# Norm scales spread by a repeated column, and shifted starts for the weight blocks that move

## The chip, the cores and the metric

One core of one Trainium2 chip runs the whole program. The metric is device time in microseconds (us) of one execution. The engines are TensorE (PE; its weight loads stand apart as PEld), VectorE (DVE), ScalarE (ACT), GpSimd (POOL) and the DMA queues, of which SyncE (SP) issues most.

## What is computed

Two transformer-like blocks run one after the other on 1024 tokens of 1024 channels, all in float32. The parts of the reference that the change touches are the root-mean-square norms and some of the projections:

```python
def rms_norm(x, w):
    xf = x.astype(jnp.float32)
    y = xf * lax.rsqrt(jnp.mean(xf * xf, axis=-1, keepdims=True) + EPS)
    return (y * w.astype(jnp.float32)).astype(x.dtype)
...
    proj = u @ w_in[l]              # first block: one slice, ib, is a value projection
...
    return rms_norm(h, final_norm_w)          # end of the first block
...
    h = rms_norm_2(x, pre1_w[l]) * (1.0 + sc1) + sh1   # start of the second
    z = h @ w_in                    # gv and mv are value projections
...
    y = swiglu_ffn(h, ffn_w_in[l], ffn_w_out[l])
    x = x + (1.0 + gt2) * rms_norm_2(y, post2_w[l])
```

The norm that ends the first block and the norm that starts the second follow each other directly, so the second one's scale depends on the first one's.

## The kernel before

Channels lie on the 128 partitions and tokens along the free axis, in two halves of 512 tokens (`H`). Four phases follow each other: A (first block's mixer), C (its output projection, gate and final norm), B (second block's mixer) and F (its feed-forward part). The order on TensorE is the order in which the code is written. The other engines are ordered by a scheduler.

**Products.** A float32 number is split into a high and a low part, `hi` and `lo`, both stored in the one-pass type `F32R`. A product takes three matmuls into the same bank: high by high, high by low, low by high (`mm3`, and by hand in `vgroup` and `vg`). In the profile `mm<-rh,hi` names the moving operand first and the stationary one second. In most products the weights are stationary in blocks of 128x128, and 512 tokens of activations (`rh`, `rl`) move.

**Blocks that move.** Three kinds of projection want their result with tokens on the partitions: the values `v` (phase A, `vgroup`), `gv` and `mv` (phase B, `vg`). There the activations are stationary in blocks of 128 tokens, and the weights move, 256 columns in a matmul (280 for `gv` of the first pair, which carries 24 columns more). One such group has 8 token blocks x 8 channel blocks x 3 matmuls = 192 matmuls. There are six groups, five of 256 and one of 280 columns, 1152 matmuls in all. The rest of the matmuls of 256 columns stand in phase F and move activations (`ah`, `al`).

**The ring.** `load_split` fetches a block of weights by DMA to `raw`, ACT copies it to `hi`, and DVE subtracts to make `lo`. `hi` and `lo` come from a ring of four buffers each, 128x1024. In the built program each buffer starts at a multiple of 64 bytes.

**Norm scales.** `token_sums` turns a tile of squares (128x512) on TensorE and adds up on DVE, which gives a column of four sums per partition. `rsqrt_cols` makes the scale of them: a `TENSOR_SCALAR` on DVE and a power on POOL (`mhalf` holds -0.5). `to_rows` spreads this column along the free axis on all partitions: DVE multiplies the identity by the column to the tile `dg` (in the profile `C<-ident,...` or `B<-ident,...`, L2597), and TensorE multiplies a matrix of ones by it (`sm<-C,ones`). The matmul is of full float32 and shows as two records. `norms` at the end of phase C needs two scales, one after the other: the second sum has to be multiplied by the first scale twice before its own power. The waits that `yield` stands for put other TensorE work between the steps.

**The end.** The last product of phase F (`XV`, entries 6 and 7) runs over two quarters of the first half, 256 tokens each. `finish` makes the norm of each quarter. There the sums of squares come from matmuls of the squares by one column of ones, five for each of two token blocks. The last call (`tail`) has no other work beside it: the squares, the sums, the power, `to_rows`, four steps of multiply and add on DVE and the output DMAs follow each other.

`warm` issues matmuls of ones by ones into a bank that nobody reads.

Of the kernel before, what the change touches and what calls it, by code (L numbers as in the profile page):

```python
# [8 lines left out]
F32 = mybir.dt.float32  # L9
F32R = mybir.dt.float32r  # L10
U32 = mybir.dt.uint32
AF = mybir.ActivationFunctionType
ALU = mybir.AluOpType
# [3 lines left out]
P = 128  # L17
# [1515 lines left out]
class PhaseC:  # L1533
# [56 lines left out]
    def phase_c(self, yh, yl):  # L1590
# [104 lines left out]
            accum(acc2[half], m, hh, scale=self.col("final_norm_w", m))  # L1695


        wfa = br.tile([P, 8], F32, name="wfa")
        r1 = br.tile([P, NCH], F32, name="r1")
        r2 = br.tile([P, NCH], F32, name="r2")  # L1700
        rb12 = pair(br, "rb12")
        self.x2d = [tc.dram_tile([P, T], F32, name=f"x2d{k}") for k in range(8)]
        x1 = self.x1 = []
# [1 line left out]
        def norms(half):  # L1705
            if not x1:

                self.stt(wfa, self.mods[:, 8:16], 1.0, self.col("pre1_w_2", 0, 8), ALU.add, ALU.mult)
                self.mul(wfa, wfa, self.col("final_norm_w", 0, 8))
                x1.extend(self.moving())  # L1710
            hs = slice(half * H, half * H + H)
            hr = slice(half * 4, half * 4 + 4)
            for _ in range(4):
                yield
            self.token_sums(r1[:, hr], acc1[half])
            self.token_sums(r2[:, hr], acc2[half])
            self.rsqrt_cols(r1[:, hr], r1[:, hr], 1.0 / D, EPS, rtmp[:, hr])
            self.mul(r2[:, hr], r2[:, hr], r1[:, hr])
            self.mul(r2[:, hr], r2[:, hr], r1[:, hr])
            self.rsqrt_cols(r2[:, hr], r2[:, hr], 1.0 / D, EPS, r2[:, hr])  # L1720
            self.mul(r2[:, hr], r2[:, hr], r1[:, hr])
            yield
            yield
            self.to_rows(rb12[half], r2[:, hr], 4)
            for k in range(8):
                t = B_()
                s = self.mods[:, k : k + 1]
                self.stt(t, h[k][:, hs], wfa[:, k : k + 1], rb12[half], ALU.mult, ALU.mult)
                self.act(x1[0][k][half], t, AF.Identity, bias=s)
                self.stt(x1[1][k][half], t, s, x1[0][k][half].bitcast(F32), ALU.add, ALU.subtract)  # L1730

        def store_x2(half):
            hs = slice(half * H, half * H + H)
            if half == 0:
                for _ in range(4):
                    yield
            rb1 = br.tile([P, H], F32, tag=f"acc1{half}", name=self.name("rb1"))
            self.to_rows(rb1, r1[:, half * 4 : half * 4 + 4], 4)
            for k in range(8):
                t = B_()  # L1740
                self.stt(t, h[k][:, hs], self.col("final_norm_w", k), rb1, ALU.mult, ALU.mult)
                (nc.sync if k % 2 else nc.gpsimd).dma_start(self.x2d[k][:, hs], t)
                yield
# [26 lines left out]
class PhaseF:  # L1770
# [58 lines left out]
    def variant(self, n, g, v):  # L1829

        if n == 0:
            self.fetch_raws(-1)
        hi = self.ring.tile([P, 1024], F32R, tag="hi", name=self.name("hi"))
        lo = self.ring.tile([P, 1024], F32R, tag="lo", name=self.name("lo"))
        if v[0] == "A" and len(v) == 2:
            self.split(hi, lo, self.raws["g", 2 * g + int(v[1])])
        else:
            if v == "S1":
                self.sl[g] = self.base.tile([P, T], F32, tag="rmask", name=self.name("sl"))
            for i in range(2):  # L1840
                c = slice(i * H, i * H + H)
                j = 2 * g + i
                up, s = self.raws["u", j], self.sl[g][:, c]
                gate = self.raws.get(("g", j))
                if v == "S1":
                    self.add(s, up[:, :H], up[:, H:])
                elif v == "S2":
                    self.sub(s, s, gate[:, :H])
                elif v == "S4":
                    self.sub(s, gate[:, H:], s)  # L1850
                elif v == "S3":
                    s = self.fl.tile([P, H], F32, tag="s3", name=self.name("s3"), bufs=1)
                    self.sub(s, gate[:, :H], up[:, :H])
                else:
                    s = up[:, H:]
                self.split(hi[:, c], lo[:, c], s)
        self.fetch_raws(n)
        return hi, lo
# [12 lines left out]
    def variant2(self, v, e):  # L1871
        n = (2 if e < 5 else 1) * H
        if v == "S1":
            s = self.sc[e] = self.sp.tile([P, n], F32, tag=f"sc{e}", name=f"sc{e}")
            a, b = self.quad(1, 0, e), self.quad(1, 1, e, "ru")
            self.add(s, a, b)
        elif v in ("S2", "S4"):
            s, a = self.sc[e], self.quad(0, v == "S4", e)
            if v == "S2":
                self.sub(s, s, a)  # L1880
            else:
                self.sub(s, a, s)
        elif v == "S3":
            s = self.quad(1, 1, e)
            self.sub(s, s, self.sc[e])
        else:
            s = self.quad(int(v[1]) - 1, int(v[2]) - 1, e)
        hi = self.ring.tile([P, 1024], F32R, tag="hi", name=self.name("hi"))
        lo = self.ring.tile([P, 1024], F32R, tag="lo", name=self.name("lo"))
        self.split(hi[:, :n], lo[:, :n], s)  # L1890
        return hi, lo

    def phase_f(self, x):
# [327 lines left out]
        def finish(t0, t1, sq=None):  # L2221
            n = t1 - t0
            half, o = t0 // H, t0 % H
            hr = slice(t0 // P, t1 // P)
            rb = tp.tile([P, H], F32, tag="rb", name=self.name("rb"))[:, :n]
            per, xs = 1024 // n, []
            for i in range(8 // per):
                t = tp.tile([P, 1024], F32, tag=f"sc{i + o // 128}", name=self.name("X")).rearrange("p (m t) -> p m t", m=per)
                xs.append(t)
                for m in range(per):  # L2230
                    nc.sync.dma_start(t[:, m], self.x3d[i * per + m][:, t0:t1])
            tail = t1 == H
            if not tail:
                yield
            if t1 == 256:
                yield
            if sq is None:
                yield from self.rstd_rows(accs[half], rt[:, hr], rtmp[:, hr], rb, 1)
            else:

                ps = self.sm_ps()
                for j in range(n // P):
                    c = slice(j * P, j * P + P)
                    for m in range(5):
                        src = accs[0][:, o + j * P : o + j * P + P] if m == 0 else sq[:, m - 1, c]
                        self.mm(ps[:, j : j + 1], src, self.ones[:, 0:1], m == 0, m == 4)
                self.rsqrt_cols(rt[:, hr], ps[:, : n // P], 1.0 / D, EPS, rtmp[:, hr])
                yield
                r = self.to_rows(None if tail else rb, rt[:, hr], n // P)
                rb = r if tail else rb  # L2250
            parts = [(0, 2), (2, 2), (4, 2), (6, 2)]
            if tail:
                parts[3:] = [(6, 1), (7, 1)]
            for m0, k in parts:
                y = outs(m0 // 4, half)[:, m0 % 4 : m0 % 4 + k, o : o + n]
                x = xs[m0 // per][:, m0 % per : m0 % per + k]
                self.mul(y, y, rb.unsqueeze(1).broadcast_to([P, k, n]))
                self.add(y, y, x)
                nc.sync.dma_start(self.out[m0 : m0 + k, :, t0:t1].rearrange("m p t -> p m t"), y)
                if t1 == T:  # L2260
                    yield
# [77 lines left out]
class Stream:  # L2339
# [14 lines left out]
    def more(self):  # L2354
        if self.next < len(self.seq):
            key, src, n = self.seq[self.next]
            self.next += 1
            self.tiles[key] = src() if callable(src) else self.k.load_split(src, n)

    def get(self, key):  # L2360
        return self.tiles[key]
# [8 lines left out]
class K(PhaseA, PhaseB, PhaseC, PhaseF):  # L2370
# [145 lines left out]
        self.act(hi, src, AF.Copy)  # L2516
        self.sub(lo, src, hi.bitcast(F32))

    def load_split(self, src, n=1024):
        raw = self.raw_tile()  # L2520
        hi = self.ring.tile([P, 1024], F32R, tag="hi", name=self.name("hi"))
        lo = self.ring.tile([P, 1024], F32R, tag="lo", name=self.name("lo"))
        dst = raw[:, :n]
        if len(src.shape) == 3:
            dst = dst.rearrange("p (k c) -> p k c", k=src.shape[1])
# [67 lines left out]

    def to_rows(self, out, colt, n):

        dg = self.C_().rearrange("p (n c) -> p n c", n=4)[:, :n, :]
        self.nc.vector.tensor_tensor(  # L2597
            out=dg, in0=self.ident.unsqueeze(1).broadcast_to([P, n, P]), in1=colt.unsqueeze(2).broadcast_to([P, n, P]),
            op=ALU.mult,
        )  # L2600
        ps = self.sm_ps()[:, : n * P]
        self.mm(ps, self.ones, dg.rearrange("p n c -> p (n c)"))
        if out is None:
            return ps
        self.act(out, ps, AF.Copy)
# [26 lines left out]
```

## Time and profile before

| | us |
|---|---|
| median of three runs (2165.47, 2168.87, 2169.49) | 2168.87 |
| the profiled execution | 2165.11 |
| its span in the trace | 2163.4 |
| TensorE busy in the span | 2129.4 |
| VectorE busy | 1497.7 |
| ScalarE busy | 915.3 |
| GpSimd busy | 118.6 |

The span runs from the first to the last instruction that the trace holds, and 1.7 us lie around it. TensorE is busy 98% of the span, which counts a matmul from its start to the end of its flow through the array. Matmuls overlap, so the pace is read from the distance between starts, not from the length of one.

### The profile page before, as it was taken

How to read it: one execution, taken by the hardware profiler on the slowest of the kernel's cores; microseconds unless marked ns; L12 is line 12 of the kernel's file. 1: busy time of each engine (PE TensorE's matmuls, PEld its weight loads, DVE VectorE, ACT ScalarE, POOL GpSimd, SP SyncE). 2: the span in 40 equal slices, each digit the busy share in tenths (PEclk: the TensorE clock that was granted, in tenths of full speed). 3: DMA queues.
4: the chain of work that ended last, by engine and by line, in shares of the span. 5: the costliest groups of instructions: out<-in, count | busy, mean ns of one | idle time of the engine just before them, and what ended most of it. 6: DMA issues, size and time to landing. Idle time of an engine off the chain costs nothing.

```text
span 2163.4 us, 29412 instructions
## 1 busy us (share of the span) xinstructions
PE 2129.4 (98%) x11050; PEld 1768.7 (82%) x11050; DVE 1497.7 (69%) x2306; ACT 915.3 (42%) x1542; POOL 118.6 (5%) x210
## 2 busy tenths in 40 slices
PE   9999999999999999999999999999999999999997
PEld 7988888887799898787787778887878888878887
DVE  7675687676576633567757345848997876769987
ACT  5544453443345544525254222346632232334454
POOL 1000000000212110000000000001000000000000
PEclk9999999999999999999999999999999999999998
DMA  5110116421364334346554456655534422258645
GB/s 180 30 42 33 52 31 196 134 79 39 128 201 119 104 107 147 131 132 209 176 186 137 142 179 196 189 167 175 163 133 152 137 88 88 73 200 291 204 149 174
DMA packets 148999, 297.06 MB, mean 137 GB/s; under 512 B 21473, under 2 KB 43889, under 8 KB 148601
## 3 DMA queue, kind: packets, MB, share of 16 engines
q1 hardware_dynamic: 133016, 268.70, 38.6%
q0 software_dynamic: 8128, 20.07, 2.7%
q10 hardware_dynamic: 7712, 6.41, 1.0%
q8 instruction: 87, 1.43, 0.3%
q14 instruction: 56, 0.45, 0.1%
HBM read 229.93 MB, written 64.00 MB: 136 GB/s over the span
## 4 chain that ended last, share of the span: by engine, by line
PE 88%; DVE 5%; DMA 3%; issue 2%; ACT 2%; POOL 0%; SPq 0%; POOLq 0%; ACTq 0%; DVEq 0%
PE mm L2503 65%; PE sm L2503 21%; PE sm L2512 1%; DVE lo L2471 1%; DVE rl L2483 0%; DVE B L2483 0%; ACT C L2497 0%; DMA mD<-mlrows 0%; DVE res L2483 0%; DMA s5y<-s5d 0%; ACT T L2497 0%; DVE adaa L2483 0%; DMA raw<-in_wfi 0%; DVE mq L2483 0%; DMA ru<-in_wfi 0%
## 5 line engine op out<-in xcount | busy, mean ns | idle before, releaser
L2503 PE MATMUL mm<-rh,hi 128*128 128x512 f32 x1552 | 623.2, 402 | 1.1 <-DVE c L2471 0.8
L2503 PE MATMUL mm<-rh,lo 128*128 128x512 f32 x1552 | 605.4, 390 | 0.0
L2503 PE MATMUL mm<-rl,hi 128*128 128x512 f32 x1552 | 604.8, 390 | 0.0
L2503 PEld LDWEIGHTS mm<-rh,hi 128*128 128x128 f32 x1552 | 291.5, 188 | 71.1 <-issue 8.3
L2503 PEld LDWEIGHTS mm<-rh,lo 128*128 128x128 f32 x1552 | 291.3, 188 | 62.2
L2503 PEld LDWEIGHTS mm<-rl,hi 128*128 128x128 f32 x1552 | 291.8, 188 | 59.1 <-issue 3.1
L2497 ACT ACTIVATE hi<-raw 128x1024 fp32r<-128x1024 f32 (+2 forms) x189 | 182.9, 970 | 355.5 <-PE mm L2503 270.3
L2471 DVE TENSOR_TENSOR lo<-raw,hi 128x1024 fp32r<-128x1024 f32 (+2 forms) x189 | 209.9, 1113 | 95.5 <-ACT hi L2497 93.8
L2503 PE MATMUL mm<-yr,hi 128*128 128x512 f32 x384 | 118.6, 390 | 0.2 <-DVE yr L2483 0.2
L2503 PE MATMUL mm<-hi,rh 128*128 128x256 f32 (+1 forms) x384 | 110.7, 288 | 0.0
L2503 PE MATMUL mm<-hi,rl 128*128 128x256 f32 (+1 forms) x384 | 109.2, 284 | 0.0
L2503 PE MATMUL mm<-lo,rh 128*128 128x256 f32 (+1 forms) x384 | 109.2, 284 | 0.0
L2503 PE MATMUL mm<-tv,hi 128*128 128x512 f32 x312 | 97.3, 394 | 3.1 <-ACT tv L2497 3.1
L2483 DVE SCALAR_TENSOR_TENSOR adaa<-adar,cact,adaa 128x512 f32<-128x512 f32 x84 | 63.0, 750 | 36.8 <-DMA adar<-in_adaw 36.1
L2503 PEld LDWEIGHTS mm<-yr,hi 128*128 128x128 f32 x384 | 72.1, 188 | 15.9 <-DVE yr L2483 1.0
L2497 ACT ACTIVATE hi<-sl 128x512 fp32r<-128x512 f32 x66 | 39.5, 627 | 106.7 <-DVE sl L2471 60.4
L2503 PEld LDWEIGHTS mm<-hi,rh 128*128 128x128 f32 x384 | 73.4, 191 | 1.7 <-issue 1.2
L2503 PE MATMUL mm<-yr,lo 128*128 128x512 f32 x192 | 74.7, 389 | 0.0
L2503 PEld LDWEIGHTS mm<-hi,rl 128*128 128x128 f32 x384 | 73.4, 191 | 0.7 <-issue 0.2
L2503 PEld LDWEIGHTS mm<-lo,rh 128*128 128x128 f32 x384 | 73.4, 191 | 0.0
L2503 PEld LDWEIGHTS mm<-tv,hi 128*128 128x128 f32 x312 | 59.2, 190 | 15.9 <-ACT tv L2497 3.5
L2503 PE MATMUL sm<-tv,hi 128*128 128x512 f32 x216 | 66.5, 389 | 0.0
(513 smaller groups left out, 3922.3 us busy)
## 6 DMA issues: line engine op xcount, KB each, us to landing
raw<-in_w SPq DMA_DIRECT2D x60, 512.0 KB
adar<-in_adaw SPq DMA_DIRECT2D x96, 256.0 KB
raw<-in_wfo SPq DMA_DIRECT2D x40, 512.0 KB
c<-ffa SPq DMA_DIRECT2D x69, 256.0 KB
raw<-in_wfi SPq DMA_DIRECT2D x34, 512.0 KB
raw<-in_wo SPq DMA_DIRECT2D x24, 512.0 KB
ru<-in_wfi SPq DMA_DIRECT2D x22, 512.0 KB
raw<-in_wpj SPq DMA_DIRECT2D x32, 256.0 KB
```

What stands on the lines that cost most here:

```text
L2471: self.nc.vector.tensor_tensor(out=out, in0=a, in1=b, op=op)
L2483: self.nc.vector.scalar_tensor_tensor(out=out, in0=a, scalar=s, in1=b, op0=op0, op1=op1)
L2497: self.nc.scalar.activation(out=out, in_=a, func=f, scale=scale, **kw)
L2503: self.nc.tensor.matmul(out, lhsT=l, rhs=r, start=start, stop=stop)
L2512: self.nc.tensor.transpose(out, a, self.ident[:n, :n])
```

## The change

Four edits.

- `to_rows` no longer makes `dg`. It issues one matmul for each 128 tokens, with the identity moving, and as stationary operand one column of scales, repeated 128 times by a step of zero.
- `norms` makes both scales from the two sums at once: with a = s1/D + EPS, the first scale is a to the power -1/2, and the second scale times the first is (s2/D + EPS * a) to the power -1/2. Two `TENSOR_SCALAR` and one `SCALAR_TENSOR_TENSOR` on DVE and a single power of eight columns on POOL stand where two powers with DVE steps between them stood.
- In `finish` for the two quarters, the sums by a column of ones become ten turns (`is_transpose`) that add up in one bank, square by square, and a `TENSOR_REDUCE` on DVE. At the tail, `warm(6)` comes ahead of them and `warm(5)` behind them.
- The ring's tiles have 1040 columns instead of 1024. Blocks whose key is `v`, `gv` or `mv` start four columns (16 bytes) into their tile, all others at its start. A tile is now 4160 bytes long, so all others still start at a multiple of 64 bytes.

```diff
@@ norms
-            self.token_sums(r1[:, hr], acc1[half])
-            self.token_sums(r2[:, hr], acc2[half])
-            self.rsqrt_cols(r1[:, hr], r1[:, hr], 1.0 / D, EPS, rtmp[:, hr])
-            self.mul(r2[:, hr], r2[:, hr], r1[:, hr])
-            self.mul(r2[:, hr], r2[:, hr], r1[:, hr])
-            self.rsqrt_cols(r2[:, hr], r2[:, hr], 1.0 / D, EPS, r2[:, hr])
-            self.mul(r2[:, hr], r2[:, hr], r1[:, hr])
+            r = r12[half]
+            for q, sums in enumerate((acc1, acc2)):
+                self.token_sums(r[:, q], sums[half])
+            self.ts(t12[:, 0], r[:, 0], 1.0 / D, EPS)
+            self.ts(t12[:, 1], t12[:, 0], EPS)
+            self.stt(t12[:, 1], r[:, 1], 1.0 / D, t12[:, 1], ALU.mult, ALU.add)
+            flat = "p q n -> p (q n)"
+            nc.gpsimd.tensor_tensor(out=r.rearrange(flat), in0=t12.rearrange(flat), in1=self.mhalf, op=ALU.pow)
             yield
             yield
-            self.to_rows(rb12[half], r2[:, hr], 4)
+            self.to_rows(rb12[half], r12[half][:, 1], 4)
@@ finish
-                ps = self.sm_ps()
-                for j in range(n // P):
-                    c = slice(j * P, j * P + P)
-                    for m in range(5):
+                ps = self.sm_ps()[:, :n]
+                if tail:
+                    self.warm(6)
+                for m in range(5):
+                    for j in range(n // P):
+                        c = slice(j * P, j * P + P)
                         src = accs[0][:, o + j * P : o + j * P + P] if m == 0 else sq[:, m - 1, c]
-                        self.mm(ps[:, j : j + 1], src, self.ones[:, 0:1], m == 0, m == 4)
-                self.rsqrt_cols(rt[:, hr], ps[:, : n // P], 1.0 / D, EPS, rtmp[:, hr])
+                        nc.tensor.matmul(
+                            ps[:, c], lhsT=src, rhs=self.ident, is_transpose=True, start=m == 0 and j == 0, stop=m == 4 and j == n // P - 1
+                        )
+                nc.vector.tensor_reduce(
+                    out=rt[:, hr], in_=ps.rearrange("p (n c) -> p n c", c=P), axis=mybir.AxisListType.X, op=ALU.add
+                )
+                self.rsqrt_cols(rt[:, hr], rt[:, hr], 1.0 / D, EPS, rtmp[:, hr])
                 yield
+                if tail:
+                    self.warm(5)
                 r = self.to_rows(None if tail else rb, rt[:, hr], n // P)
@@ Stream.more
-            self.tiles[key] = src() if callable(src) else self.k.load_split(src, n)
+            shift = 4 if key[0] in ("v", "gv", "mv") else 0
+            self.tiles[key] = src() if callable(src) else self.k.load_split(src, n, shift)
@@ new, used by load_split, variant and variant2
+    def ring_pair(self, shift=0):
+        t = [self.ring.tile([P, 1040], F32R, tag=q, name=self.name(q)) for q in ("hi", "lo")]
+        return [q[:, shift : shift + 1024] for q in t]
@@ to_rows
-        dg = self.C_().rearrange("p (n c) -> p n c", n=4)[:, :n, :]
-        self.nc.vector.tensor_tensor(
-            out=dg, in0=self.ident.unsqueeze(1).broadcast_to([P, n, P]), in1=colt.unsqueeze(2).broadcast_to([P, n, P]),
-            op=ALU.mult,
-        )
         ps = self.sm_ps()[:, : n * P]
-        self.mm(ps, self.ones, dg.rearrange("p n c -> p (n c)"))
+        for j in range(n):
+            self.mm(ps[:, j * P : (j + 1) * P], colt[:, j : j + 1].broadcast_to([P, P]), self.ident)
```

The shift of the weight blocks changes no order. The other edits do; two places follow. On DVE in `norms` of the first half (phase C), `r` stands for both sums and their scales, `C_4393` is `dg`, and the rows of `C`, `res` and `lo` between belong to the gate products; before:

```order
L2585 TENSOR_REDUCE r_3517<-sm_4331 128x4
L2585 TENSOR_REDUCE r_3518<-sm_4337 128x4
L2489 TENSOR_SCALAR rtmp_c<-r_3517 128x4
L2471 TENSOR_TENSOR r_3518<-r_3518,r_3517 128x4 x2
L2471 TENSOR_TENSOR C_4369<-mm_4312,rb_2804 128x512
L2489 TENSOR_SCALAR r_3518<-r_3518 128x4
L2471 TENSOR_TENSOR lo_4365<-raw_4363,hi_4364 128x1024
L2471 TENSOR_TENSOR r_3518<-r_3518,r_3517 128x4
L2483 SCALAR_TENSOR_TENSOR C_4369<-C_4369,sm_4356 128x512
L2483 SCALAR_TENSOR_TENSOR res_2799<-C_4369,res_2799 128x512
L2597 TENSOR_TENSOR C_4393<-ident,r_3518 128x512
```

The same stretch of DVE after, with `t_3521` the column that the power reads:

```order
L2599 TENSOR_REDUCE r_3519<-sm_4336 128x4
L2599 TENSOR_REDUCE r_3519<-sm_4342 128x4
L2499 TENSOR_SCALAR t_3521<-r_3519 128x4
L2497 TENSOR_SCALAR t_3521<-t_3521 128x4
L2493 SCALAR_TENSOR_TENSOR t_3521<-r_3519,t_3521 128x4
L2481 TENSOR_TENSOR C_4371<-mm_4317,rb_2806 128x512
L2481 TENSOR_TENSOR lo_4367<-raw_4365,hi_4366 128x1024
L2493 SCALAR_TENSOR_TENSOR C_4371<-C_4371,sm_4358 128x512
L2493 SCALAR_TENSOR_TENSOR res_2801<-C_4371,res_2801 128x512
```

All DVE steps of the scale now stand directly behind the sums, ahead of the 128x512 and 128x1024 work, and the row of `dg` is gone.

On PE at the very end, behind the last product's matmuls; before, with `sq` the four squares, `acc` the older sum of squares and `mm_18723` the spread scale:

```order
L2503 MATMUL sm_18470<-ah_18603,lo_18555 128x256
L2503 MATMUL mm_18708<-ones,acc_16581 128x1
L2503 MATMUL mm_18708<-ones,sq_18684 128x1 x4
L2503 MATMUL mm_18708<-ones,acc_16581 128x1
L2503 MATMUL mm_18708<-ones,sq_18684 128x1 x4
L2503 MATMUL mm_18723<-C_18721,ones 128x256
```

After:

```order
L2513 MATMUL sm_18478<-ah_18612,lo_18563 128x256
L2513 MATMUL mm_18717<-ones 128x128 x6
L2247 MATMUL mm_18716<-ident,acc_16588 128x128 x2
L2247 MATMUL mm_18716<-ident,sq_18692 128x128 x8
L2513 MATMUL mm_18737<-ones 128x128 x5
L2513 MATMUL mm_18743<-ident,rt_f 128x128 x2
```

Both token blocks of one square are now taken together, so only two turns stand behind the last square, where before all five matmuls of the second block stood there; eleven matmuls that nobody reads are new.

## Rows read from the trace of the kernel before

**Rows 1.** The page: busy time by engine, and the chain that ended last.

```profile
PE 2129.4 (98%) x11050; PEld 1768.7 (82%) x11050; DVE 1497.7 (69%) x2306; ACT 915.3 (42%) x1542; POOL 118.6 (5%) x210
...
PE 88%; DVE 5%; DMA 3%; issue 2%; ACT 2%; POOL 0%; SPq 0%; POOLq 0%; ACTq 0%; DVEq 0%
```

**Rows 2.** Weight loads (count, busy us, mean ns): under 512, then 256 columns.

```profile
L2503 PEld LDWEIGHTS mm<-rh,hi 128*128 128x128 f32 x1552 | 291.5, 188 | 71.1 <-issue 8.3 <-DVE c L2471 1.2 <-DVE res L2471 0.7
...
L2503 PEld LDWEIGHTS mm<-hi,rh 128*128 128x128 f32 x384 | 73.4, 191 | 1.7 <-issue 1.2
```

**Rows 3.** PE timeline (start us, length us, operation): 39 matmuls of 256 columns.

```profile
53.04 0.28 PE L2503 MATMUL mm<-hi,rh 128*128 128x256 f32 x1
...
57.60 0.28 PE L2503 MATMUL mm<-lo,rh 128*128 128x256 f32 x1
```

**Rows 4.** PE timeline, 512 columns: ten matmuls.

```profile
480.43 0.39 PE L2503 MATMUL mm<-rh,hi 128*128 128x512 f32 x1
...
482.47 0.39 PE L2503 MATMUL mm<-rh,hi 128*128 128x512 f32 x1
```

**Rows 5.** PE timeline, 280 columns: nine matmuls, then six from other ring buffers.

```profile
604.62 0.29 PE L2503 MATMUL mm<-hi,rh 128*128 128x280 f32 x1
...
605.77 0.29 PE L2503 MATMUL mm<-hi,rh 128*128 128x280 f32 x1
...
606.56 0.29 PE L2503 MATMUL mm<-hi,rh 128*128 128x280 f32 x1
```

**Rows 6.** PE's waits: who waited for whom, us in total, times, longest.

```profile
PE mm L2503 <- ACT tv L2497: 3.1, 1, 3.1
...
PE sm L2503 <- DVE C L2597: 2.3, 2, 1.8
...
PE sm L2503 <- DVE B L2597: 0.5, 1, 0.5
```

**Rows 7.** Timeline in phase C, all engines: the turns, the second power, `dg`, the spread.

```profile
515.79 1.03 PE L2512 MATMUL sm<-ident,acc 128*128 128x128 f32 x8
...
520.03 1.91 POOL L2592 TENSOR_TENSOR r<-r,mhalf 128x4 f32<-128x4 f32 x1 [1.15 <-DVE r L2489]
...
523.38 0.68 DVE L2597 TENSOR_TENSOR C<-ident,r 128x512 f32<-128x512 f32 x1
...
524.12 1.12 PE L2503 MATMUL sm<-C,ones 128*128 128x512 f32 x2 [1.83 <-DVE C L2597]
```

**Rows 8.** The powers on POOL: ns min/median/max, forms.

```profile
L2592 POOL TENSOR_TENSOR rt_f<-rtmp_f,mhalf x7: 695/1007/1041, 1456.1 to 2152.9; 128x4 f32<-128x4 f32 x5, 128x2 f32<-128x2 f32 x2
```

**Rows 9.** DVE writes to `D`, starts at 0 and at 12 bytes into a tile mixed.

```profile
L2471 DVE TENSOR_TENSOR D<-mm,rb_a x37: 682/687/694, 44.8 to 325.0; 128x512 f32<-128x512 f32 x37
```

**Rows 10.** Timeline of PE: the sums of the first of the two quarters.

```profile
2137.77 0.28 PE L2503 MATMUL mm<-ones,acc 128*128 128x1 f32 x2
2137.91 1.03 PE L2503 MATMUL mm<-ones,sq 128*128 128x1 f32 x8
...
2139.92 0.36 PE L2503 MATMUL sm<-ah,hi 128*128 128x256 f32 x1
```

**Rows 11.** Timeline of the tail, all engines: squares, DVE steps, PE's spread.

```profile
2150.25 0.71 ACT L2497 ACTIVATE sq<-y 128x256 f32<-128x256 f32 x2
...
2152.62 0.16 DVE L2489 TENSOR_SCALAR rtmp_f<-mm 128x2 f32<-128x2 f32 x1 [2.47 <-PE mm L2503]
...
2153.59 0.42 DVE L2597 TENSOR_TENSOR C<-ident,rt_f 128x256 f32<-128x256 f32 x1 [0.81 <-POOL rt_f L2592]
...
2154.07 1.22 PE L2503 MATMUL mm<-C,ones 128*128 128x256 f32 x2 [1.48 <-DVE C L2597]
...
2155.33 1.29 DVE L2471 TENSOR_TENSOR y<-y,mm 128x512 f32<-128x512 f32 x2 [1.31 <-PE mm L2503]
```

**Rows 12.** Stretches of the tail: us, busy by engine, PEclk, DMA share, GB/s.

```profile
2148.00:2151.00 3.00, 1.63 (x13) 1.42 (x11) 2.16 (x6) 1.80 (x6) 0.00 (x0) 1.00 0.62 209
...
2154.00:2156.00 2.00, 1.22 (x2) 0.50 (x2) 0.69 (x3) 0.00 (x0) 0.00 (x0) 0.50 0.00 0
```

More of the change, by code (lines that the diff above doesn't have):

```diff
@@ L1698, in phase_c @@
         wfa = br.tile([P, 8], F32, name="wfa")
-        r1 = br.tile([P, NCH], F32, name="r1")
-        r2 = br.tile([P, NCH], F32, name="r2")
+        r12 = [br.tile([P, 2, 4], F32, name=f"r12{j}") for j in range(2)]
+        t12 = br.tile([P, 2, 4], F32, name="t12")
         rb12 = pair(br, "rb12")
@@ L1711, in norms @@
             hs = slice(half * H, half * H + H)
-            hr = slice(half * 4, half * 4 + 4)
             for _ in range(4):
                 yield
-            self.token_sums(r1[:, hr], acc1[half])
-            self.token_sums(r2[:, hr], acc2[half])
-            self.rsqrt_cols(r1[:, hr], r1[:, hr], 1.0 / D, EPS, rtmp[:, hr])
-            self.mul(r2[:, hr], r2[:, hr], r1[:, hr])
-            self.mul(r2[:, hr], r2[:, hr], r1[:, hr])
-            self.rsqrt_cols(r2[:, hr], r2[:, hr], 1.0 / D, EPS, r2[:, hr])
-            self.mul(r2[:, hr], r2[:, hr], r1[:, hr])
+            r = r12[half]
[6 more added lines that the diff above has]
+            nc.gpsimd.tensor_tensor(out=r.rearrange(flat), in0=t12.rearrange(flat), in1=self.mhalf, op=ALU.pow)
             yield
             yield
-            self.to_rows(rb12[half], r2[:, hr], 4)
+            self.to_rows(rb12[half], r12[half][:, 1], 4)
             for k in range(8):
@@ L1737, in store_x2 @@
             rb1 = br.tile([P, H], F32, tag=f"acc1{half}", name=self.name("rb1"))
-            self.to_rows(rb1, r1[:, half * 4 : half * 4 + 4], 4)
+            self.to_rows(rb1, r12[half][:, 0], 4)
             for k in range(8):
@@ L1832, in variant @@
             self.fetch_raws(-1)
-        hi = self.ring.tile([P, 1024], F32R, tag="hi", name=self.name("hi"))
-        lo = self.ring.tile([P, 1024], F32R, tag="lo", name=self.name("lo"))
+        hi, lo = self.ring_pair()
         if v[0] == "A" and len(v) == 2:
@@ L1887, in variant2 @@
             s = self.quad(int(v[1]) - 1, int(v[2]) - 1, e)
-        hi = self.ring.tile([P, 1024], F32R, tag="hi", name=self.name("hi"))
-        lo = self.ring.tile([P, 1024], F32R, tag="lo", name=self.name("lo"))
+        hi, lo = self.ring_pair()
         self.split(hi[:, :n], lo[:, :n], s)
@@ L2517, in split, with load_split @@
         self.sub(lo, src, hi.bitcast(F32))
-    def load_split(self, src, n=1024):
+    def ring_pair(self, shift=0):
+        t = [self.ring.tile([P, 1040], F32R, tag=q, name=self.name(q)) for q in ("hi", "lo")]
+        return [q[:, shift : shift + 1024] for q in t]
+    def load_split(self, src, n=1024, shift=0):
         raw = self.raw_tile()
-        hi = self.ring.tile([P, 1024], F32R, tag="hi", name=self.name("hi"))
-        lo = self.ring.tile([P, 1024], F32R, tag="lo", name=self.name("lo"))
+        hi, lo = self.ring_pair(shift)
         dst = raw[:, :n]
```

## The prediction

> **What bounds the kernel now.** I read the page first: TensorE is busy 98% of the span and holds 88% of the chain that ended last [rows 1]. So an edit pays in one of two ways: TensorE does its work at a quicker pace, or one of its few waits goes. The list of PE's waits comes next. It is short: the largest that the edits can reach are the two for `dg` (2.3 us together, the longer 1.8), one for `dg` under the name B (0.5) and one of 3.1 for the activations `tv` of phase F [rows 6]. Then I read the pace of the matmuls from the distance of their starts. Of 256 moving columns, 39 matmuls start within 4.56 us, 120.0 ns apart [rows 3]. Of 512, ten start within 2.04 us, 226.7 ns apart [rows 4]. The 256 columns between them take 106.7 ns, which is one column per cycle at 2.4 GHz, so every matmul of either length carries 13.3 ns that its columns don't explain. Last comes the tail, where nothing runs beside the chain [rows 11].
>
> **The shifted starts.** 1152 matmuls move shifted blocks, 960 of 256 and 192 of 280 columns. What the start of a block is worth no row shows, since all blocks start at multiples of 64 bytes. But three rows say that place matters. At 280 columns nine matmuls are 127.8 ns apart and the next six, of other ring buffers, 131.7 [rows 5]; the columns alone take 116.7. So the excess is 11.1 in one place and 15.0 in another, for the same shape. And weight loads last 191 ns under these moving blocks, 188 under 512 columns [rows 2]: loading and moving seem to hinder each other. The bounds for a gain: zero, and the pace of weight loads alone, which matmuls of one moving column show: twenty records from 2137.77 to 2139.92 are 2.15/20 = 0.108 us apart [rows 10]. That leaves 12 ns at most, 1152 x 12 = 13.8 us. On the other side the place could turn out worse; that is a rival below. I take 4 ns, under the middle, since the two rows nearest to it are the 3.9 ns between the two places [rows 5] and the 3 ns of the loads [rows 2]: 1152 x 4 = 4.6 us, all on the path, since TensorE waits for nothing in these stretches. What writes the blocks stays hidden: 26 copies and subtractions, and DVE's writes that start 12 bytes into a tile mix with aligned ones within 682 to 694 ns [rows 9].
>
> The Trainium skill speaks against this edit (TensorE: Matmul & The Clock Gate, section "Step-by-step: what each phase is for"): TensorE reads moving and stationary operands through two independent ports, so that loading weights takes no read bandwidth from a running matmul. By that, a new start gives nothing and the term is 0 instead of -4.6. The longer loads of [rows 2] lean the other way, weakly. The same page (section "Back-to-back issue gap") puts a warm matmul at N/2.4 + 2.5 ns, 109.2 for 256 columns, an estimate by that page that would make the term 1152 x 10.8 = 12.4 us; the 120.0 of [rows 3] does not agree with it as things stand.
>
> **The scales of phase C.** TensorE reaches the first half's spread at 524.12 - 1.83 = 522.29 and waits 1.83 us for `dg` [rows 7]. Before it stood two powers with DVE steps between them: the second began at 520.03, 1.15 us after the first had ended, and was stretched to 1.91 us beside DVE's work. After the change one power starts where the first did, two small DVE steps later, at about 518.1. Its length isn't in the trace: 695 ns for two columns and 1007 for four [rows 8] give 156 a column, so 1.63 us for eight, and 3.1 if stretched by the same factor as the 1.91. It ends between 519.7 and 521.2, ahead of 522.29. The wait goes whole: -1.8. What is late next is the wait for the last squares of the other half some 18 us on, which hangs on TensorE's own products and moves with them. The wait for B, 0.5 us [rows 6], is for a `dg` that stood in DVE's row although its scale was long there: -0.5. The second of the two waits for C is 2.3 - 1.8 = 0.5 in phase F and goes likewise: -0.5.
>
> **`tv` in phase F.** TensorE waits 3.1 us for an activation that DVE's and ACT's work behind the last norm makes. A `dg` of 0.68 us [rows 7] goes from DVE ahead of it: -0.6 if DVE is the bound there, 0 if not. I take -0.6.
>
> **The spread itself on TensorE.** The old one takes 1.12 us in two records from start to end [rows 7]. The new one has eight records of 128 columns; paced by weight loads at 0.108, with a last one of some 0.28 (as [rows 3]), that is 7 x 0.108 + 0.28 = 1.04, or 1.23 with a first load in the open. Taken at +0.05 for each of eleven: +0.5. A stationary operand with step zero isn't in the trace; it could load in 0 to 188 ns more [rows 2], and I take 0.
>
> **The two quarters.** The first quarter's sums hold TensorE from 2137.77 to 2139.92, 2.15 us [rows 10]. Ten turns, paced as the eight of [rows 7], (1.03 - 0.28)/7 = 0.107, take 1.07, with the step back to the product some 1.25: -0.9, on the path. The new `TENSOR_REDUCE` on DVE is covered by the product that TensorE goes on with; uncovered it would cost some 0.4 us.
> In the tail the last square ends at 2150.96 and its sum is read at 2152.62, 1.66 us later [rows 11]. Now two turns (0.11 + 0.28, and a load of up to 0.19) and a reduce of about 0.42, the length of `dg` with its 256 columns, stand there: 1.0, so -0.7. From `dg`'s start at 2153.59 to DVE's next step at 2155.33 it is 1.74 us; four records take 3 x 0.108 + 0.28 and a load, 0.8 at 2.4 GHz, or about 1.3 at the 1.2 GHz that the stretch shows (0.50 of full clock) [rows 12]. The `warm` matmuls run while ACT makes squares and POOL the power; at 1.2 GHz the five behind could last 0.6 us too long. I take the middle: -0.7.
>
> **The sum.** Scales and spread: -1.8 - 0.5 - 0.5 - 0.6 + 0.5 - 0.9 - 0.7 - 0.7 = -5.2 us, between -3 (waits partly found again, tail at half clock) and -7. With the starts, -4.6: -9.8. The profiled execution took 2165.11 us, 3.76 below the median of 2168.87; the three runs lie at both of these levels. I set the base between the two, at 2167.0: **2157.2 us**. A measurement can tell about 0.2%, 4.3 us, from no change.
>
> **The rivals.**
> - *The start doesn't matter.* The matmuls stay at 120 ns, and only -5.2 is left: 2161.8. For it: 280-column blocks start at 0 and at 32 bytes in turn, and nine matmuls of both kinds are at 127.8 on average, no slower than the six of both kinds behind them [rows 5]. Against it: the two places of those rows differ at all.
> - *The start costs.* If the moving operand is read in pieces of 64 bytes, 106.7/16 = 6.7 ns each at 256 columns, a shifted block has a broken piece at each end, and both cost a full one: +13.3 ns, 1152 x 13.3 = 15.3 us, less 5.2: 2177.1. It decides from 4.5 ns a matmul (no gain left) and 8.3 ns (slower by over 0.2%). For it: the 13.3 ns excess is itself two such pieces. Against it: 280 columns are 17.5 pieces and their mean excess is no higher.
> - *A small cost*, up to 4.5 ns a matmul: 2162 to 2167.
> - *The repeated column loads slowly*, so that the spread doesn't get shorter: some 92 loads of 188 ns more each are 17.3 us, in all 2174.5. Nothing in the trace speaks for it.
>
> **How the numbers follow.** Forecast 0.50, start without effect 0.30, small cost 0.10, start costs 0.08, slow column 0.02. The range leaves out the last two and the outermost of the first: from 2150.5 (9 of the 12 ns for the starts, -10.4, and -6 for the rest) to 2168.0 (small cost, upper level of the runs). Faster by over 0.2%: nearly all of the forecast and 0.7 of the second case, where -5.2 is close to the bound of 4.3: 0.70. Slower: the last two, 0.10. The same: 0.20.
>
> **What would show it.** In the changed kernel's trace: 256-column matmuls of `hi` and `lo` 116 ns apart while those of `ah` stay at 120 (right), or 120 (the second case) or 125 and more (the costly ones); loads back at 188 ns; no wait of PE at the spread in phase C; a power of 1.6 to 3.1 us there; from the last square to DVE's first multiply of the tail 3 us instead of 4.4; PEclk near 1.00 until the last spread. The forecast is wrong if the pace of the shifted blocks doesn't move, or if the wait of phase C returns at the next turns.

## The result, and the profile after

The changed kernel takes 2180.6 us (median of four runs, 2179.3 to 2183.0) against 2167.2 for the kernel before, measured beside it: ratio 1.0065, 95% interval 1.0052 to 1.0078. It is slower by 0.65%, some 13 us, where 2157.2 was forecast. The profiled execution took 2182.97 us, its span is 2181.3, against 2163.4 before. So 17.9 us of span have to be found. That is more than the 13 of the medians because the profiled execution of the kernel before lay 2.1 us under its median and that of the changed kernel 2.4 over its own.

The page of the kernel after, busy time and chain:

```profile
PE 2154.2 (99%) x11134; PEld 1777.3 (81%) x11134; DVE 1491.0 (68%) x2289; ACT 915.1 (42%) x1542; POOL 116.7 (5%) x208
...
PE 87%; DVE 4%; DMA 3%; ACT 2%; issue 2%; SPq 0%; ACTq 0%; POOLq 0%; POOL 0%; DVEq 0%
```

TensorE is busy 24.8 us longer and waits less (27.1 us of the span not busy, 34.0 before). DVE and POOL have less to do. So the time went into the matmuls. The next view is TensorE's timeline in phase C: first and last matmul of four products of 512 moving columns (start us, length us), 24, 16 (the last of 24), 24 and 24 matmuls.

```profile
469.20 0.39 PE L2513 MATMUL mm<-rh,hi 128*128 128x512 f32 x1
...
474.57 0.39 PE L2513 MATMUL mm<-rh,lo 128*128 128x512 f32 x1
...
478.01 0.39 PE L2513 MATMUL mm<-rh,lo 128*128 128x512 f32 x1
...
481.41 0.40 PE L2513 MATMUL mm<-rh,lo 128*128 128x512 f32 x1
...
490.29 0.39 PE L2513 MATMUL mm<-rh,hi 128*128 128x512 f32 x1
...
495.55 0.39 PE L2513 MATMUL mm<-rh,lo 128*128 128x512 f32 x1
...
497.14 0.40 PE L2513 MATMUL mm<-rh,hi 128*128 128x512 f32 x1
...
502.50 0.40 PE L2513 MATMUL mm<-rh,lo 128*128 128x512 f32 x1
```

The distances of starts are 5.37/23 = 233.5 ns, 3.40/15 = 226.7, 5.26/23 = 228.7 and 5.36/23 = 233.0. Before, all stood at 226.7 [rows 4]. The four products have their stationary blocks in the four different buffers of the ring. The built program says what differs. Before, the ring's tiles are 4096 bytes long, and in all one-pass matmuls of 512 and 256 columns the start of the stationary block lies a multiple of 256 bytes from the start of what moves against it. Now the tiles are 4160 bytes long, and the four buffers lie 0, 64, 128 and 192 bytes (modulo 256) from it. I call this the **distance**. The products above have 64, 0, 192 and 128. None of these blocks is one that the change shifts. With the whole trace laid beside the built program in order, the back-to-back matmuls of 512 columns start 228.1, 233.2, 232.6 and 229.4 ns apart on the mean at distances of 0, 64, 128 and 192.

The times between all successive starts, summed over both traces, give the account. For 512 columns (some 7270 pairs that start less than 300 ns apart) the mean went from 227.3 to 230.7 ns, and the sum by +22.9 us; the trace after has eight such pairs fewer, and their 1.8 us stand in the last term. For 256 columns it went from 120.9 to 119.3: -1.7 us. 280 columns: 129.2 and 129.4. All that is left (waits, turns, spreads, short matmuls): -3.1 us. That is +18.1 us, against 17.9 of span; behind TensorE's last start the trace after is 0.3 us shorter.

Of the forecast's own signs most came, and one failed: the matmuls of `ah` and `al`, which were to stay at 120 ns, went from a mean of 120.2 to 117.8, though the change doesn't shift them. The timeline of a group of shifted matmuls, 39 distances from the first line to the last, 4.60/39 = 117.9 ns (120.0 in [rows 3]):

```profile
53.56 0.28 PE L2513 MATMUL mm<-hi,rh 128*128 128x256 f32 x1
...
58.16 0.28 PE L2513 MATMUL mm<-hi,rh 128*128 128x256 f32 x1
```

The page's group of weight loads under such matmuls (count, busy us, mean ns), 188 ns as against 191 in [rows 2]:

```profile
L2513 PEld LDWEIGHTS mm<-hi,rh 128*128 128x128 f32 x384 | 72.3, 188 | 1.4 <-issue 1.0
```

The timeline in phase C, the power of eight columns and the spread, which no longer waits (compare [rows 7]):

```profile
524.65 1.64 POOL L1722 TENSOR_TENSOR r<-t,mhalf 128x8 f32<-128x8 f32 x1 [97.29 <-DVE t L2493]
...
528.59 1.05 PE L2513 MATMUL sm<-ident,r 128*128 128x128 f32 x8
```

PE's three longest waits of the whole run (total us, times, longest; compare [rows 6]):

```profile
PE mm L2513 <- DVE al L2481: 3.2, 1, 3.2
PE mm L2513 <- DVE w L2481: 3.0, 1, 3.0
PE sm L2522 <- DVE mhn L2481: 2.9, 2, 2.5
```

The timeline of the first quarter's sums on PE, and of the tail (compare [rows 10, 11]):

```profile
2158.42 0.38 PE L2247 MATMUL mm<-ident,acc 128*128 128x128 f32 x2
...
2159.43 0.36 PE L2513 MATMUL sm<-ah,hi 128*128 128x256 f32 x1
...
2169.72 0.71 ACT L2507 ACTIVATE sq<-y 128x256 f32<-128x256 f32 x2
...
2170.96 0.42 DVE L2250 TENSOR_REDUCE rt_f<-mm 128x2 f32<-128x256 f32 x1 [1.33 <-PE mm L2247]
2171.42 0.17 DVE L2499 TENSOR_SCALAR rtmp_f<-rt_f 128x2 f32<-128x2 f32 x1
...
2171.66 0.69 POOL L2606 TENSOR_TENSOR rt_f<-rtmp_f,mhalf 128x2 f32<-128x2 f32 x1 [10.38 <-DVE rtmp_f L2499]
...
2172.41 0.71 PE L2513 MATMUL mm<-ident,rt_f 128*128 128x128 f32 x4 [0.38 <-POOL rt_f L2606]
2173.16 1.29 DVE L2481 TENSOR_TENSOR y<-y,mm 128x512 f32<-128x512 f32 x2 [1.58 <-PE mm L2513]
```

The stretch that holds the last spread (us, busy by engine, PEclk, DMA, GB/s; compare [rows 12]):

```profile
2172.00:2174.00 2.00, 0.75 (x5) 0.52 (x4) 0.84 (x2) 0.00 (x0) 0.36 (x1) 1.00 0.00 0
```

### The profile page after: what moved, and what is told of

Read it like the earlier page. It is cut to its first block, busy times and chain, and to the rows that moved or that the text cites. A ratio compares the mean times of both kernels' runs of the same rounds, so it can differ in the third digit from the quotient of the medians.

```text
span 2181.3 us, 29569 instructions
## 1 busy us (share of the span) xinstructions
PE 2154.2 (99%) x11134; PEld 1777.3 (81%) x11134; DVE 1491.0 (68%) x2289; ACT 915.1 (42%) x1542; POOL 116.7 (5%) x208
## 4 chain that ended last, share of the span: by engine, by line
PE 87%; DVE 4%; DMA 3%; ACT 2%; issue 2%; SPq 0%; ACTq 0%; POOLq 0%; POOL 0%; DVEq 0%
PE mm L2513 65%; PE sm L2513 21%; PE sm L2522 1%; DMA mD<-mlrows 1%; DVE lo L2481 1%; DMA adar<-in_adaw 1%; ACT hi L2507 0%; ACT e L2507 0%; DVE rl L2493 0%; DVE adaa L2493 0%; DMA raw<-in_wfo 0%; DMA s5y<-s5d 0%; DVE mq L2493 0%; DMA ru<-in_wfo 0%; DVE B L2493 0%
```

## The experiments

The theory after this reading: the ring's longer tiles, not the shift and not the norms, cost the time, because the pace of a row of matmuls depends on the distance between its two operands. Rivals: the shift itself costs, the norm edits cost, or a block's own place matters. All ratios below are to the kernel before, run on the same chip.

**A bare scan of the distance** (m1_scan). One core, nothing but rows of 32 matmuls in one bank:

```python
for i, (n, mo, d) in enumerate(CONFIGS):       # columns, moving start, distance (bytes)
    m = mov[:, mo // 4 : mo // 4 + n]
    for j in range(32):
        s = (mo + d) // 4 + (j % 8) * 128
        matmul(ps[:, :n], lhsT=sta[:, s : s + 128], rhs=m, start=j == 0, stop=j == 31)
```

> This kernel leaves the whole computation out: it only issues rows of 32 matmuls on one core, stationary blocks 512 bytes apart, one fixed moving tile, and copies input to output. Between rows the distance d from the start of the moving operand to the start of the stationary one goes through 0 to 496 bytes in steps of 16, for 512, 256 and 280 moving columns, and the moving operand itself starts at 0, 16, 64, 128 or 192 bytes. Theory (distance): the pace depends on d modulo 256 and not on where the moving operand starts: 512 columns 227 ns at d = 0, 233 at 64, 232 at 128, 229 at 192; 256 columns 120 at 0 and 113 at 192. Rival (place): the pace depends on the stationary operand's own place, so that rows with d = 0 but a start at 64 or 128 bytes are as slow as those with d = 64 or 128. Rival (no address effect): all rows of one length have one pace, 227 and 120.

The timeline, 31 matmuls of a row in each line (start, length of them all): 512 columns at distances 0, 32, 64, 128, 192; then moving start and block both at 128 bytes; then 256 columns at 0, 64, 192 and 240.

```profile
27.65 7.19 PE L45 MATMUL c<-mov,sta 128*128 128x512 f32 x31
...
42.16 7.39 PE L45 MATMUL c<-mov,sta 128*128 128x512 f32 x31
...
57.09 7.39 PE L45 MATMUL c<-mov,sta 128*128 128x512 f32 x31
...
86.93 7.39 PE L45 MATMUL c<-mov,sta 128*128 128x512 f32 x31
...
116.70 7.40 PE L45 MATMUL c<-mov,sta 128*128 128x512 f32 x31
...
294.62 7.21 PE L45 MATMUL c<-mov,sta 128*128 128x512 f32 x31
...
390.48 3.88 PE L45 MATMUL c<-mov,sta 128*128 128x256 f32 x31
...
405.82 3.68 PE L45 MATMUL c<-mov,sta 128*128 128x256 f32 x31
...
436.15 3.82 PE L45 MATMUL c<-mov,sta 128*128 128x256 f32 x31
...
447.39 3.88 PE L45 MATMUL c<-mov,sta 128*128 128x256 f32 x31
```

Without the last matmul's own length (0.39 and 0.28 us), 30 distances are left. At 512 columns that is (7.19 - 0.39)/30 = 226.7 ns at 0, and 233.3 at 32, 64, 128 and 192. The row with both operands 128 bytes further on is at 227.3, so the block's own place is not what counts; the pattern repeats after 256 bytes (226.7 at 256 too). 16 bytes gave 226.7 as well, 240 gave 227.0 and 176 gave 230. It is not quite clean: at 192 three rows with other moving starts had 228.9, and with a moving start at 16 bytes a distance of 0 had 229.9 and one of 192 had 226.7. So for moving starts off a multiple of 64 bytes the distance alone doesn't settle the pace. At 256 columns: 120.0, 113.3, 118.0, 120.0. The 280-column rows lay between 126.6 and 130.0. So the number of columns decides which distance is good: 0 is the best for 512 and among the worse ones for 256. At 240 and 176, where four fifths of the shifted 256-column blocks lie in the changed kernel, the scan had 120 and 118: little or nothing won.

**The norm edits alone** (e1_norms_alone): ring tiles of 1024 columns again, no shift.

```diff
-        t = [self.ring.tile([P, 1040], F32R, ...) for q in ("hi", "lo")]
+        t = [self.ring.tile([P, 1024], F32R, ...) for q in ("hi", "lo")]
-            shift = 4 if key[0] in ("v", "gv", "mv") else 0
+            shift = 0 if key[0] in ("v", "gv", "mv") else 0
```

> All edits of the change but the ring's: tiles of 1024 columns, no shift. Theory (distance between operands): the 512-column matmuls are back at 227.3 ns, and only the norm edits are left, 2162 us, some 5 below the kernel before. Rival (the norm edits cost): 2167 or more, with new waits of TensorE behind the powers or the spreads.

Measured 2159.4 us, ratio 0.9956 (0.9941 to 0.9971). The norm edits gain 9.5 us (6 to 13), rather more than the 5 expected; the spans of the two profiled executions differ by 4.2 (2159.2 and 2163.4).

**The longer tiles alone** (e2_pitch_alone): the kernel before, with

```diff
-        hi = self.ring.tile([P, 1024], F32R, tag="hi", ...)
+        hi = self.ring.tile([P, 1040], F32R, tag="hi", ...)[:, :1024]
```

and `lo` alike, in all places.

> The kernel before with ring tiles of 1040 columns, of which the last 16 are never used; nothing is shifted, no norm is edited. Theory (distance): buffers two to four of the ring move by 64, 128 and 192 bytes against the moving tiles, so the 512-column matmuls go to a mean of 231 ns, +23 to +26 us, and the 256-column ones get quicker by 2 to 4 ns, -2 to -4 us: 2187 to 2191 in all. Rival (the shifted starts cost, or the norm edits): no change, 2167.

Measured 2187.8 us, ratio 1.0091 (1.0076 to 1.0106), some 19 us more, for 16 columns that nobody writes or reads. The sum over starts gives +22.9 us for 512 columns, to the tenth what the changed kernel shows, and -2.1 for 256. One group of the 512-column matmuls (count, busy us, mean ns of one), here and then in the kernel before:

```profile
L2503 PE MATMUL mm<-rl,hi 128*128 128x512 f32 x1552 | 609.9, 393 | 0.0
```

```profile
L2503 PE MATMUL mm<-rl,hi 128*128 128x512 f32 x1552 | 604.8, 390 | 0.0
```

The 3 ns show in the mean length too, in both kernels with long tiles (610.0, 393 in the changed one). The two rivals that put the loss on the shift or on the norms have fallen. This run and the last add up to some 9.5 us more; the whole change cost 13, and the intervals, 3 us to each side, leave room for the difference.

**The shift without the uneven tiles** (e3_shift16_even_pitch, then 64 bytes). `hi` and `lo` of a slot share a tile of 8448 bytes, 33 x 256; the room comes from a mask's scratch tile.

```diff
-        t = [self.ring.tile([P, 1040], F32R, tag=q, ...) for q in ("hi", "lo")]
-        return [q[:, shift : shift + 1024] for q in t]
+        t = self.ring.tile([P, 2112], F32R, tag="hilo", ...)
+        return [t[:, o + shift : o + shift + 1024] for o in (0, 1024)]
```

> The changed kernel with hi and lo of a ring slot in one tile of 2112 columns (8448 bytes, 33 times 256), so that all blocks which are not shifted keep a distance to the moving tiles that is a multiple of 256 bytes; the shifted blocks still begin 16 bytes in. Theory (distance): 512 columns at 227.3 ns, shifted blocks at 117 to 118, so norms -5 and starts -2 to -3: about 2160. Rival (the shift of 16 bytes itself costs): 2175 to 2181, with the 512-column matmuls still at 231.

Measured 2161.6 us, ratio 0.9967 (0.9955 to 0.9979). The change as it was meant is some 20 us faster than as it was built. But it doesn't beat the norm edits alone. Against the kernel before, the 256-column mean fell by 1.6 ns, 1.7 us in all; against the run of the norm edits alone the shifted blocks of 256 columns gained 2.1 us by the sum over starts, 2.3 ns each, and those of 280 columns nothing. Against it stand longer waits of TensorE than in that run, for `w` 4.4 us instead of 3.0 and for `acc` 3.8 instead of 2.3; the shared tile is the likely cause.

With `shift = 16` instead of 4 (e4_shift64_even_pitch):

> As the run with a 16-byte shift and an even pitch (2161.6 us), but the shifted blocks begin 64 bytes in, so that the stationary start lies 192 bytes (modulo 256) from the moving one. Theory (distance): the bare rows of 256 columns gave two paces there, 113.3 and 117.8 ns, where a distance of 240 gave 113.3 to 119.9: 960 matmuls at 1.5 to 6 ns less than the 119.3 of the 16-byte run, -1.4 to -5.8 us, so 2156 to 2160. 512 columns stay at 227.3. Rival (a start that is a multiple of 64 bytes is like no shift at all, and only the distance of nothing matters): the 256-column matmuls stay at 120, 2161 to 2163.

2160.0 us, ratio 0.9962 (0.9950 to 0.9975). The shifted matmuls had a mean of 118.7 ns, nearly all at 117 to 119, 109 of 936 at 113 and 114: mostly the slower of the two paces that the scan had led to expect. The time is 1.6 us under the 16-byte run, which the intervals don't tell from nothing.

Then `ah` and `al` of phase F 64 bytes in as well (e5_shift64_ah_too), and the same with `hi` and `lo` in tiles of their own again, 4352 bytes (17 x 256), the room taken from `ones` (64 columns) and from one of three `C` buffers of phase A (e6_separate_tiles):

```diff
-        t = self.ring.tile([P, 2112], F32R, tag="hilo", ...)
+        t = [self.ring.tile([P, 1088], F32R, tag=q, ...) for q in ("hi", "lo")]
```

> As the run with the 64-byte shift, and the two-quarter activations of the last phase (ah, al, 256 columns) begin 64 bytes into their tiles as well. Theory (distance): some 240 more matmuls at 2 to 6.7 ns less, -0.5 to -1.6 us against the 64-byte run. Rival (no effect of the moving start): the same time.

> As the run before it in this list, but hi and lo stand in tiles of their own again (1088 columns, 4352 bytes, 17 times 256); room comes from a smaller tile of ones and two instead of three C buffers in the first phase. Theory (distance, and the common tile of hi and lo costs the 2 us by which the 16-byte run stood above the norm edits alone): 512 columns at 227.3, 256 columns at 113 to 118, 2152 to 2157, the fastest of all. Rival (the common tile costs nothing): the same as the run with ah shifted.

2158.9 us, ratio 0.9961 (0.9948 to 0.9973): the step for `ah` is too small to be seen in the time; the mean over all 256-column matmuls fell to 118.5 ns. And 2154.7 us, ratio 0.9944 (0.9931 to 0.9958) with separate tiles: the wait for `w` is back at 3.0, for `acc` at 2.3. This is the fastest version, 12 us below the kernel before and 26 below the changed one.

**What picks the pace at 256 columns** (m2_history): rows of 48 as in the first scan, behind rows of other lengths.

> Leaves the whole computation out, as the first bare scan: rows of 48 matmuls on one core. Rows of 256 columns at a distance of 0, 64 or 192 bytes are each entered behind rows of another kind (512 columns at distance 0 or 64, 136, 264 or 300 columns at distance 0), with the moving operand at 0 or 64 bytes. Theory (the 256-column pace has several steady states, and the way into a row picks one): at a distance of 64 and of 192 some rows hold 113.3 ns and others 117.8 to the end, for the same distance; at 0 all hold 120. Rival (the moving operand's own place decides): rows with the same place and distance have one pace whatever stands ahead.

The timeline, 47 matmuls a line, all with 256 columns and a distance of 64, entered behind 512 columns at distance 64, 136 columns, 264 columns and 512 columns at distance 0:

```profile
106.02 5.49 PE L46 MATMUL c<-mov,sta 128*128 128x256 f32 x47
...
116.83 5.70 PE L46 MATMUL c<-mov,sta 128*128 128x256 f32 x47
...
128.24 5.51 PE L46 MATMUL c<-mov,sta 128*128 128x256 f32 x47
...
156.98 5.70 PE L46 MATMUL c<-mov,sta 128*128 128x256 f32 x47
```

(5.49 - 0.28)/46 = 113.3 ns, then 117.8, 113.7 and 117.8, for one and the same shape and place; 113.7 is a mean that settles at 113.3. With the moving operand and the block both 64 bytes further on, rows behind 512 columns at distance 0 and behind 264 columns gave 117.8 and 113.7 again, so what stands ahead decided, not the moving operand's place. At a distance of 0 all rows held 120. At 192 all held 117.8, so that half of the theory did not show. Rows behind 512 columns at distance 0, as they stand in this kernel, come in at 117.8.

Whether 64 would still do better in the kernel (e7_shift192, blocks and `ah` 192 bytes in):

> As the run with tiles of their own and 64-byte starts (2154.7 us), with starts at 192 bytes instead, so that the distance is 64 modulo 256. Theory (distance): in the run with the wide ring tiles alone, 256-column matmuls at a distance of 64 had a mean of 115.9 ns against 118.4 at 192; 1200 x 2.6 = 3.1 us less, 2151 to 2153. Rival (the mean of 115.9 came from what stood ahead of those rows, not from the distance): 118.5 ns and 2154.7 again.

2156.1 us, ratio 0.9950 (0.9938 to 0.9961), mean 118.3 ns: the rival. This fits the bare scan, in which the pace at a distance of 64 went with what stood ahead; for the 115.9 of the run with long tiles itself it isn't shown.

**The tail without warm matmuls** (e8_no_warm), on top of the norm edits alone:

```diff
-                if tail:
-                    self.warm(6)
...
-                if tail:
-                    self.warm(5)
```

> All edits of the change but the ring's, and without the eleven matmuls of warm in the tail. If they are what keeps TensorE's clock up: the granted clock of the last spread falls to 0.5 and its start-to-DVE time grows by 0.4 to 0.6 us against the run of the norm edits alone. Rival (the shorter tail keeps the clock by itself): granted clock near 1.00 at the spread and the same length, or even shorter by what the warm matmuls hold up.

Without warm, the timeline of the spread and DVE's next step:

```profile
2149.66 1.22 PE L2509 MATMUL mm<-ident,rt_f 128*128 128x128 f32 x4 [1.49 <-POOL rt_f L2602]
2150.91 1.28 DVE L2477 TENSOR_TENSOR y<-y,mm 128x512 f32<-128x512 f32 x2 [2.09 <-PE mm L2509]
```

The stretch that holds the spread (columns as above), without warm and then in the run of the norm edits alone:

```profile
2149.60:2151.00 1.40, 1.22 (x4) 0.93 (x4) 0.09 (x1) 0.00 (x0) 0.00 (x1) 0.50 0.00 0
```

```profile
2150.30:2151.20 0.90, 0.71 (x4) 0.52 (x4) 0.12 (x1) 0.00 (x0) 0.00 (x0) 1.00 0.00 0
```

The granted clock is 0.50, the lower of its two levels (1.2 GHz), and the four records take 1.22 us instead of 0.71. The warm matmuls are worth 0.5 us in the tail, as the theory said. Over the whole run it doesn't show: the spans are 2159.0 us without them and 2159.2 with them, since without them the last product ended 0.7 us earlier, for a cause that wasn't looked for. Time of the single run: 2160.7 us.

**All blocks of the ring off by the same amount** (e9_all_16, e10_all_32), on the fastest version:

```diff
-        return [q[:, shift : shift + 1024] for q in t]
+        return [q[:, 4 : 4 + 1024] for q in t]      # second run: 8
```

> As the fastest run so far (2154.7 us), but every block of the ring begins 16 bytes into its tile, those that stand still as well, so that 7248 of the 512-column matmuls have a distance of 16 bytes. Theory (distance modulo 256, by the bare scan: 226.7 ns at 0 and 16, 233.4 from 32 on): 512 columns stay at 227.3, 2154 to 2158. Rival (a start off a multiple of 64 bytes costs by itself): 7248 times 2 to 6 ns, 2169 or more.

> The same with every block of the ring 32 bytes into its tile, a distance of 32 for 7248 of the 512-column matmuls. Theory (distance, by the bare scan): 233.4 instead of 226.7 ns, 7248 times 6.6 is 48 us more, 2200 to 2204; none of these kernels' tiles has moved otherwise. Rival (the loss of the changed kernel came from something else that the 4160-byte tiles moved): 2154 to 2158.

32 bytes: 2193.1 us, ratio 1.0128 (1.0112 to 1.0143). The mean at 512 columns went to 233.0 ns, 40 us over the fastest version by the sum over starts; the time rose by 38. The edit also moves the blocks that were shifted by 64 bytes, which changed the sum at 256 columns by less than 0.5 us in either run. The time came 7 us under the range, mostly since I took the whole step from 226.7 to 233.4, while the kernel's mean starts at 227.3. 16 bytes: 2179.5 us, ratio 1.0058 (1.0046 to 1.0071). Here my expectation was wrong: the mean is 230.8 ns, not 227.3. The timeline of that run shows why, two successive products of 24 matmuls with the same ring buffers, over the first and the second half of the tokens (first and last of each):

```profile
473.78 0.39 PE L2513 MATMUL mm<-rh,hi 128*128 128x512 f32 x1
...
479.00 0.39 PE L2513 MATMUL mm<-rh,lo 128*128 128x512 f32 x1
...
481.05 0.40 PE L2513 MATMUL mm<-rh,hi 128*128 128x512 f32 x1
...
486.42 0.40 PE L2513 MATMUL mm<-rh,lo 128*128 128x512 f32 x1
```

5.22/23 = 227.0 ns and 5.37/23 = 233.5, at the same distance. So 16 bytes has both paces, and the bare scan had shown one of them. Its number for the rival, 2169 or more, is what came; but a start off a multiple of 64 doesn't explain it by itself, since whole products with it run at 227. What chose between the two paces here wasn't tested.

## Why the prediction was wrong, step by step

**The term that was missing.** The forecast gave the starts of the shifted blocks a price and the ring's longer tiles none. The sentence that failed is "What the start of a block is worth no row shows, since all blocks start at multiples of 64 bytes": from the same modulo 64 it was silently concluded that the blocks which are not shifted stay where they were. They moved by 64, 128 and 192 bytes. In the built program 5472 of the 7632 matmuls of 512 columns, those of three buffers in four, changed their distance to what moves against them, nearly five times as many as the shifted ones. One ns on these is 5.5 us. No rival had them either: all four priced the 1152 matmuls or the spreads. [rows 5] had no warning of it: by the built program both of its groups have distances of 0 and 160 bytes (the first also 64), so that its 127.8 and 131.7 ns are two paces at the same distances. They don't price a start, as I had read them. Measured, the term is +22.9 us, which alone turns a gain of some 5 into a loss of 18 in the trace.

**The shifted starts**: mis-sized, and what came isn't the shift's to claim. -4.6 us were forecast (4 ns each). In the changed kernel the shifted blocks of 256 columns gained 1.2 us (1.4 ns on the mean), those of 280 nothing, and the other 0.5 of the -1.7 is `ah` and `al`, which are not shifted. The longer tiles alone gave -2.1 without any shift. With an even pitch the shift is worth 2.1 us by the starts (2.3 ns each at 256 columns), under half of the forecast, and the time doesn't show it. The first group is 117.9 ns apart, not 116. The weight loads did fall to 188 ns, but with the longer tiles alone they did so too (188 to 189), and a shorter load turned out to be no measure of the pace.

**The scales of phase C**: right. The power takes 1.64 us (1.63 forecast), ends at 526.29, and the spread at 528.59 waits for nothing. The waits for B and for the second C are gone too: -2.8 in all. Part of it may come back elsewhere: the two waits for `mhn` grew from 1.9 to 2.9 us.

**`tv`**: wrong by 0.6. The wait of 3.1 us is still there, 3.0, now put down to DVE's `w`. The `dg` was not what held it.

**The spread**: 1.05 us from start to end against 1.12, inside the forecast 1.04 to 1.23. A column repeated by a step of zero loads as any other block here: 190 ns for the group `sm<-ident,r`, where the loads of whole blocks take 188 to 192.

**The quarters**: right or better. First quarter 2159.43 - 2158.42 = 1.01 us against 2.15, -1.1 (forecast -0.9). Tail: last square at 2170.43, sum read 0.99 us later (1.0 forecast). From the power's end to DVE's first multiply 0.81 us instead of 1.78 (it had ended at 2153.55), -1.0 (forecast -0.7, counted from the start of `dg`), with the clock at 1.00. From the last square to that multiply 2.73 us instead of 4.37; the forecast said 3.

Together the norm terms were forecast at -5.2. The two spans say -4.2, the timed runs -6 to -13. Why the timed gain is larger than the trace's was not settled; the first profiled execution of the kernel before (2165.11) lay 3.8 us under its median and that of the norm edits 1.5 over its own, which would make up most of it.

## What to carry to other kernels

Padding a tile of a ring moves every buffer behind the first. Before such an edit, list from the built program how far each stationary block starts from what moves against it, before and after, and price the matmuls whose distance changes, all of them, not only those that the edit is for. For wide moving operands (512 columns here) keep that distance at a multiple of 256 bytes, and choose tile lengths that are such multiples.

## What the runs showed of the hardware that I had not expected

- The pace of back-to-back one-pass matmuls depends on the distance between the starts of the two operands, modulo 256 bytes; this is shown for moving starts at multiples of 64 bytes. At 512 columns the bare scan had 226.7 ns at 0 and 233.3 at most other distances. The Trainium skill (TensorE: Matmul & The Clock Gate, section "Step-by-step: what each phase is for") says that the two operands are read through independent ports and that a weight load takes nothing from the running matmul; a pace that hangs on how the two operands lie to each other does not agree with that.
- Above the columns' own time (213.3 ns for 512, 106.7 for 256, at the one column per cycle of the prediction) the paces that recur lie 226.7 - 213.3 = 13.3 and 233.3 - 213.3 = 20.0 ns at 512, and 113.3 - 106.7 = 6.7 and 120.0 - 106.7 = 13.3 at 256. Other rows hold paces between, such as 228.9 or 117.8. What the excess is made of no run shows.
- At some distances a row holds one of two paces: 113.3 or 117.8 ns at 256 columns and 64 bytes, where it went with what stood ahead of the row, and 227 or 233 at 512 columns and 16 bytes, where that wasn't tried. A single row of a bare scan shows one of them; the run with all blocks at 16 bytes was mispredicted for that reason. How a row comes to its pace stays open.
